# A macaron transformer block on one core: weight and bias transfers rearranged, and the order of the mixer's first jobs

## The chip, the cores and the metric

The kernel runs on one core of a Trainium2 chip. The metric is the device time of one execution in microseconds (us). Three executions of the kernel before the change took 1017.09, 1017.39 and 1017.83 us.

## What is computed

One block, for 512 tokens of width 1024, all in float32:

```python
x = x + 0.5 * swiglu(rmsnorm(x, norm_ffn1), w_gate1, w_up1, w_down1)      # d_ff = 2816
x = x + hybrid_mixer(rmsnorm(x, norm_mix), w_in, compression weights, w_out, rel_bias)
x = x + 0.5 * swiglu(rmsnorm(x, norm_ffn2), w_gate2, w_up2, w_down2)
return rmsnorm(x, norm_final)
```

The mixer projects the normalised x with `w_in` to queries, keys and values of 16 heads of width 64. Eight heads ("moba") attend over blocks; the other eight ("nsa") have three branches (compressed, selected, window), each weighted by a gate `sigmoid(h @ w)`. The compressed branch adds learned positions (`cmp_pos_k`, `cmp_pos_v`) to windows of 32 raw keys or values, and puts each window through a two-layer net (2048 to 256 with silu, 256 to 64). Every branch adds a bias that depends on the distance of the two tokens (`rel_bias`, 32 buckets).

## The kernel before

**Arithmetic.** TensorE works on float32 split into two parts: every weight and activation tile becomes a high part (`nc.scalar.activation(..., AF.Copy)` on ScalarE) and a low part (a subtraction on VectorE). A product is three matmuls (`mm3`, lines 96 to 99: high by high, high by low, low by high). In the profile these are the lines L97, L98 and L99, whatever they compute. The split of a weight tile is `halves` (L77 to L94): `whi` on ScalarE (L88), `wlo` on VectorE (L92) or, in the attention part, on GpSimd (L90).

**Order of the work.** The kernel is traced once; a scheduler with a timeline simulation sets each engine's final order and places the waits. `tc.issue_after(ins)` ties what is issued inside it behind the instruction `ins`.

**First feed-forward net** (L485 to L538). The first four of 22 blocks of 128 hidden features are computed plainly (`plain`, L254), while `sums_of_x` and `blocks_of_x` (L207 to L232) prepare sums of x for the other 18, which go in pairs by a scheme with seven products in place of eight (`pair`, L285, 14 steps to a pair). `down` (L365) adds each finished group of four blocks to x. `go` (L420) walks over the steps, and lets transfers run 12 steps ahead of the matmuls, sums 6 and splits 4. All transfers are issued by SyncE (SP in the profile). Weight chunks of 512 KB go to the buffer `raw` (`chunk`, L66, three tiles; the plain blocks' and the down projection's weights), those of 256 KB to `aw` (16 tiles; the pairs' weights). `fetch` (L60) ties each weight transfer of the nets behind the one before it, in the order of the steps:

```python
    def fetch(to, src):
        with tc.issue_after(fetched[0].ins) if fetched[0] else nullcontext():
            fetched[0] = nc.sync.dma_start(to, src)
```

**Bias tables.** `make_rows` (L466) computes the bias over the distance and writes it to DRAM (`scr_r`, `scr_c`). From there `after` (L502), called at every step, issues eight copies of 384 KB from DRAM to DRAM (`scr_t`, L518: every row 128 times, two heads to a copy) at the steps 10, 15, ... 45, and 32 small transfers of 16 KB (`cb`, L525, four at a time) at the steps 72, 80, ... 128. They wait for the rows, and are tied to nothing else. `scr_t` is read by `bias_tile` (L789) for each head of the mixer, `cb` by `cmp_pair` (L919).

**Between net and mixer.** `then` (L532) runs for each of the eight tiles of x when the last down projection is added: it adds (L483), makes the mixer's input (`gained`, L140) and squares (L154). `rms` (L165) turns the sum of squares into 1/rms: matmuls into `pr` (L171), a square root into `rc` on ScalarE (L173; one value to a token), a reciprocal on VectorE (L174), transposes into `pR` (L177), and a copy to `R` (L178; the same values along the free axis).

**The mixer's first jobs.** `stream` (L770) takes a list of jobs, each with a weight chunk and a body of matmuls, and loads two jobs ahead. `pre` (L957) is the list until attention begins: `kproj` and `vproj` (projections, 24 matmuls of 512 columns), `vn` (three chunks of a projection whose last 24 columns are the gates), `khid` and `vhid` (four chunks each of the first layer of the compression net, about 8 matmuls of 256 columns to a chunk of 512 KB), `vm` (four chunks, 24 matmuls of 512 columns each), `ksec` and `vsec` (the second layer), `proj(10)` and `proj(12)`. Behind `kproj` and `vproj`, `blocks` (L668) multiplies by R (L570), adds the positions in eight additions of 64x248, four on GpSimd and four on VectorE (L676), into a tile that it takes from `raw`, and splits the result (`ak`, L682 and L683); only then can `khid` and `vhid` begin. `vn` ends with splits scaled by `rc` (L648, L649) and with the gates, a sigmoid on ScalarE (L651); `vm` uses the same PSUM banks.

**The rest.** Attention and the output projection are interleaved by a paced loop (L1016); the second feed-forward net has the first one's form; the final norm follows.

Of the kernel before, what the change touches and what calls it, by code (L numbers as in the profile page):

```python
# [9 lines left out]
F32 = mybir.dt.float32  # L10
F32R = mybir.dt.float32r
AF = mybir.ActivationFunctionType
# [8 lines left out]
NT = S // 128  # L21
# [3 lines left out]
RVW = 384  # L25
# [4 lines left out]
def block_kernel(ctx: ExitStack, tc: tile.TileContext, A: dict, out: bass.AP):  # L30
# [26 lines left out]

    fetched = [None]

    def fetch(to, src):  # L60

        with tc.issue_after(fetched[0].ins) if fetched[0] else nullcontext():
            fetched[0] = nc.sync.dma_start(to, src)


    def chunk(shape):  # L66
        raw = wp.tile([128, 1024], F32, name="raw", tag="raw", bufs=3)
        return raw[:, :shape[0] * shape[1]].rearrange("p (a b) -> p a b", a=shape[0])

    def load(src):  # L70
# [90 lines left out]
            nc.vector.tensor_tensor(acc, acc, s, ALU.add)  # L161

    summed = [None]

    def rms(ptag):  # L165


        with tc.high_priority():
            p = pt(ptag, "pr")
            for i in range(NT):  # L170
                summed[0] = nc.tensor.matmul(p[:, i:i + 1], acc[:, i * 128:(i + 1) * 128], ones_f[:, 0:1],  # L171
                                             start=True, stop=True)
            nc.scalar.activation(rc, p[:, :NT], AF.Sqrt, bias=eps, scale=1.0 / D)  # L173
            nc.vector.reciprocal(rc, rc)  # L174
            p = pt(ptag, "pR")
            for i in range(NT):
                nc.tensor.transpose(p[:, i * 128:(i + 1) * 128], rc[:, i:i + 1].to_broadcast([128, 128]), ident)  # L177
            nc.scalar.activation(R, p, AF.Copy)  # L178


    HT = S // 2
# [1 line left out]
    class Ffn:  # L183
# [70 lines left out]
        def plain(self, f):  # L254

            got = {}

            def loads(m):
                if first_w:
                    got[m] = first_w.pop(0)  # L260
                else:
                    got[m] = chunk((8, 128))
                    fetch(got[m], self.w[m][f])

            def halves_of(m):
                got[m] = halves(got[m])

            def run(m):
                p = got["p", m] = pt(None, "pgu")
                with tc.issue_after(summed[0].ins) if (f, m) == self.behind_rms else nullcontext():  # L270
                    for k in range(NK):
                        mm3(p, got[m][k], self.xg[k], k == 0, k == NK - 1)

            def finish():
                t = [self.t("t") for _ in range(2)]
                for m in range(2):
                    nc.vector.tensor_tensor(t[m], got["p", m], R, ALU.mult)
                nc.scalar.activation(t[0], t[0], AF.Silu)
                nc.vector.tensor_tensor(t[1], t[1], t[0], ALU.mult)
                self.kept(f, t[1])  # L280

            return [[lambda m=m: loads(m), None, lambda m=m: halves_of(m), lambda m=m: run(m), finish if m else None]
                    for m in range(2)]

        def pair(self, f):  # L285
# [52 lines left out]

            def c21(m):
                if m == 0:  # L340
                    nc.scalar.activation(out[0, 1][:, :HT], bank[0, "u"], AF.Silu, scale=-1.0)
                else:
                    gate, up = out[0, 1], out[1, 1]
                    nc.vector.scalar_tensor_tensor(up[:, :HT], bank[1, "u"], -1.0, gate[:, :HT], ALU.mult, ALU.mult)
                    nc.vector.scalar_tensor_tensor(up[:, HT:], up[:, HT:], -1.0, gate[:, HT:], ALU.mult, ALU.mult)
                    self.kept(f + 1, up)
# [138 lines left out]
    with ExitStack() as ph:  # L485
# [16 lines left out]
        def after(i):  # L502
            if i == 1:
                with tc.issue_after(made[0].ins):
                    for k in range(NK):
                        squares(hp, k, "h", 16)
                rms(None)
            if i == 3:
                make_rows()
            if 3 <= i < 7:  # L510
                ffn.sums_of_x(i - 3)
            if i == 7:
                for k in range(4):
                    ffn.blocks_of_x(k)
            if 10 <= i < 50 and i % 5 == 0:
                h = slice(2 * (i // 5) - 4, 2 * (i // 5) - 2)
                row = scr_r[h]
                nc.sync.dma_start(scr_t[h].rearrange("h p w -> p h w"),  # L518
                                  bass.AP(tensor=row.tensor, offset=row.offset,
                                          ap=[[0, 128], [RVW, 2], [1, RVW]]))  # L520
            if i >= 70 and i % 8 == 0 and (i - 72) // 8 < 8:
                a = (i - 72) // 8
                row = scr_c[0:1, :]
                for j in range(NT):
                    nc.sync.dma_start(  # L525
                        cb[a * 16:(a + 1) * 16, j],
                        bass.AP(tensor=row.tensor, offset=row.offset + 31 - 8 * j - a,
                                ap=[[CMW, 16], [16 * CMW, 8], [1, 32]]))

        xg = []  # L530

        def then(d, p):  # L532
            half_added(d, p)
            xg.append(gained(d, 1))
            squares(tmp, d, "tmp", 5)
# [6 lines left out]
    with ExitStack() as ph:  # L542
# [81 lines left out]
        def token_major(key, src, width, tiles):  # L624
# [5 lines left out]
            def chunk_of(k0):  # L630
                k1 = min(k0 + per, NK)

                def body(w):
# [11 lines left out]
                    for i in range(NT):  # L645
                        pv = p[i][:, :wide].rearrange("p (h c) -> p h c", c=64)
                        hi, lo = t[i][:, :, 0], t[i][:, :, 1]
                        nc.scalar.activation(hi, pv, AF.Copy, scale=rc[:, i:i + 1])  # L648
                        nc.vector.scalar_tensor_tensor(lo, pv, rc[:, i:i + 1], f32(hi), ALU.mult, ALU.subtract)  # L649
                        if wide < width:  # L650
                            nc.scalar.activation(gates[:, i], p[i][:, wide:width], AF.Sigmoid,  # L651
                                                 scale=rc[:, i:i + 1])
                    got[key] = t
                return src[:, k0:k1], body
            return [chunk_of(k0) for k0 in range(0, NK, per)]
# [8 lines left out]
        def compress(which):  # L664
# [3 lines left out]
            def blocks(p):  # L668
# [4 lines left out]
                for g in range(2):  # L673
                    for l in range(2):
                        for e in range(2):
                            (nc.gpsimd if g == l else nc.vector).tensor_tensor(  # L676
                                xv[half(l), 8 * e:8 * e + 8, g, 0:31], tv[half(g), l:16:2, e:e + 31],
                                pos[half(g), which, 16 * e + l:16 * e + 16:2].unsqueeze(2).to_broadcast([64, 8, 31]),
                                ALU.add)
# [87 lines left out]
                    squares(tmp, d, "t", 6)  # L767
            return A["w_o"][d][:, k0:k1], body

        def stream(jobs, ahead=2):  # L770

            loaded = []
            for j in range(len(jobs) + ahead):
# [129 lines left out]
        def cmp_pair(pair):  # L903
# [38 lines left out]
            def values():  # L942
# [11 lines left out]
        vproj, vhid, vsec = compress(1)  # L954
        vn = token_major("vn", A["w_n"], 280, vn_tiles)
        vm = token_major("vm", A["w_v"], 512, vm_tiles)
        pre = [kproj, *vn, proj(10, nsa_k("ks")), *khid[:2], vm[0], *khid[2:], vproj, vm[1], ksec,  # L957
               *vhid[:2], vm[2], *vhid[2:], vm[3], vsec, proj(12, nsa_q(0))]
        fill = [proj(11, nsa_k("kw")), *[proj(12 + i, nsa_q(i)) for i in range(1, 4)]]
        for i in range(4):  # L960
            fill += [proj(2 * i, moba_t("q", i)), proj(2 * i + 1, moba_t("k", i))]
# [223 lines left out]
```

## Time and profile before

| | |
|---|---|
| median of three executions | 1017.39 us |
| the profiled execution, its own time | 1020.17 us |
| its span in the profile | 1018.4 us |
| TensorE (PE) busy | 987.1 us, 97% |
| VectorE (DVE) busy | 775.5 us, 76% |
| ScalarE (ACT) busy | 565.2 us, 56% |
| GpSimd (POOL) busy | 146.9 us, 14% |
| DMA moved | 104.53 MB, mean 103 GB/s |
| mean granted TensorE clock | 0.992 of full |

The span is the time between the first and the last instruction of the profiled execution; 1.77 us of its own time lie around it. The first net runs until about 360 us, the mixer's first jobs from 365 to about 440, attention and output projection until about 655, the second net until about 1000. An engine's idle time costs something only where the end of the kernel hangs on that engine.

### The profile page before, as it was taken

The numbers are of one execution on the slowest core, as the hardware profiler recorded it, in microseconds if no ns is written. First come the engines' busy times: TensorE is split into PE (matmuls) and PEld (weight loads), VectorE is DVE, ScalarE is ACT, GpSimd is POOL, SyncE is SP. The second block draws the span as 40 slices with busy tenths as digits, with TensorE's granted clock in tenths as the row PEclk, the third lists the DMA queues.
The fourth block names the chain that finished last, engine by engine and source line by source line (L and its number), as shares of the span: only waits on it lengthen the run. The fifth ranks groups of instructions, "written<-read, shape, count | busy, mean of one in ns | idle before, by whom it ended". The sixth has DMA issues, their size and how long they took to land.

```text
span 1018.4 us, 17022 instructions
## 1 busy us (share of the span) xinstructions
PE 987.1 (97%) x6080; PEld 873.4 (86%) x6080; DVE 775.5 (76%) x1568; ACT 565.2 (56%) x1180; POOL 146.9 (14%) x203
## 2 busy tenths in 40 slices
PE   9989999999999998999999999999999999999996
PEld 6778899999999886787878888788899999999995
DVE  6788788887677477666888978679988887776744
ACT  6453554554444256566777777656365544444435
POOL 0000000000000001126555677300000000000002
PEclk9999999999999999999999999999999999999998
DMA  6483442232411224641111322335245332441102
GB/s 222 135 283 106 144 135 91 88 105 92 124 43 42 65 58 144 189 129 53 32 32 38 95 67 79 99 111 185 99 128 157 110 99 89 125 125 42 53 11 83
DMA packets 53513, 104.53 MB, mean 103 GB/s; under 512 B 10513, under 2 KB 19170, under 8 KB 53428
## 3 DMA queue, kind: packets, MB, share of 16 engines
q1 hardware_dynamic: 53428, 103.44, 32.8%
q8 instruction: 48, 0.79, 0.3%
q14 instruction: 37, 0.30, 0.1%
HBM read 97.98 MB, written 5.30 MB: 101 GB/s over the span
## 4 chain that ended last, share of the span: by engine, by line
PE 83%; DMA 7%; DVE 5%; ACT 2%; issue 1%; SPq 1%; POOL 0%; ACTq 0%; DVEq 0%; POOLq 0%
PE pd L99 7%; PE pd L98 7%; PE pd L97 7%; PE pu L97 7%; PE pu L99 6%; PE pu L98 6%; PE pw L97 5%; PE pw L99 5%; PE pw L98 5%; PE ps_t L878 3%; PE pp L97 3%; PE pp L98 3%; PE pp L99 3%; PE pv L97 2%; PE pv L99 2%; PE pv L98 2%
## 5 line engine op out<-in xcount | busy, mean ns | idle before, releaser
L222 ACT ACTIVATE sph<-aw 128x512 fp32r<-128x512 f32 x252 | 156.2, 628 | 145.3 <-PE pu L98 61.8
L88 ACT ACTIVATE whi<-raw 128x512 fp32r<-128x512 f32 (+2 forms) x216 | 125.1, 589 | 154.6 <-PE pd L98 71.7
L223 DVE TENSOR_TENSOR spl<-aw,sph 128x512 fp32r<-128x512 f32 x252 | 170.3, 685 | 45.8 <-ACT sph L222 44.1
L98 PE MATMUL pd<-h,whi 128*128 128x512 f32 x336 | 132.6, 395 | 0.3 <-DVE h L251 0.3
L99 PE MATMUL pd<-h,wlo 128*128 128x512 f32 x336 | 131.3, 392 | 1.5 <-DVE wlo L92 1.5
L97 PE MATMUL pd<-h,whi 128*128 128x512 f32 x336 | 129.8, 394 | 3.0 <-ACT h L250 3.0
L92 DVE TENSOR_TENSOR wlo<-raw,whi 128x512 fp32r<-128x512 f32 (+1 forms) x166 | 110.3, 674 | 27.9 <-ACT whi L88 26.4
L299 DVE TENSOR_TENSOR aw<-aw 128x512 f32<-128x512 f32 x144 | 97.8, 685 | 34.7 <-DMA aw<-in_wg 16.5
L97 PE MATMUL pu<-th,sph 128*128 128x256 f32 x432 | 121.5, 281 | 1.1 <-DVE t L335 1.1
L99 PE MATMUL pu<-th,spl 128*128 128x256 f32 x432 | 121.2, 281 | 0.0
L98 PE MATMUL pu<-tl,sph 128*128 128x256 f32 x432 | 121.2, 280 | 0.0
L483 DVE SCALAR_TENSOR_TENSOR x<-pd,x 128x512 f32<-128x512 f32 x88 | 60.3, 687 | 49.1 <-PE pd L99 48.9
L97 PEld LDWEIGHTS pu<-th,sph 128*128 128x128 f32 x432 | 81.6, 189 | 2.8 <-DVE t L335 1.5
L98 PEld LDWEIGHTS pu<-tl,sph 128*128 128x128 f32 x432 | 82.0, 190 | 1.1
L97 PE MATMUL pw<-xo,sph 128*128 128x256 f32 x288 | 80.9, 282 | 1.1 <-ACT sph L222 1.1
L99 PEld LDWEIGHTS pu<-th,spl 128*128 128x128 f32 x432 | 81.2, 188 | 0.2
L98 PE MATMUL pw<-xo,sph 128*128 128x256 f32 x288 | 80.6, 281 | 0.0
L99 PE MATMUL pw<-xo,spl 128*128 128x256 f32 x288 | 79.8, 281 | 0.2 <-DVE spl L223 0.2
L99 PEld LDWEIGHTS pd<-h,wlo 128*128 128x128 f32 x336 | 63.6, 189 | 14.8 <-DVE wlo L92 1.7
L97 PEld LDWEIGHTS pd<-h,whi 128*128 128x128 f32 x336 | 62.9, 188 | 14.7 <-ACT h L250 3.4
L98 PEld LDWEIGHTS pd<-h,whi 128*128 128x128 f32 x336 | 63.9, 190 | 11.7 <-DVE h L251 1.1
L788 POOL MEMSET tb<- 128x256 f32 x16 | 4.9, 312 | 357.0 <-PE pu L99 350.7
(244 smaller groups left out, 2515.1 us busy)
## 6 DMA issues: line engine op xcount, KB each, us to landing
aw<-in_wg SPq DMA_DIRECT2D x72, 256.0 KB, 3.3
aw<-in_wu SPq DMA_DIRECT2D x72, 256.0 KB, 3.8
raw<-in_wd1a SPq DMA_DIRECT2D x20, 512.0 KB, 5.4
raw<-in_wd2a SPq DMA_DIRECT2D x20, 512.0 KB, 5.0
raw<-in_w_a SPq DMA_DIRECT2D x16, 512.0 KB, 3.6
raw<-in_w SPq DMA_DIRECT2D x8, 512.0 KB, 4.3
raw<-in_w_o SPq DMA_DIRECT2D x32, 128.0 KB, 2.2
raw<-in_wg SPq DMA_DIRECT2D x7, 512.0 KB, 3.6
```

Of the source, the lines that this page charges most:

```text
L88: nc.scalar.activation(hi, v, AF.Copy)
L92: nc.vector.tensor_tensor(lo, v, f32(hi), ALU.subtract)
L97: nc.tensor.matmul(p, w[0], v[0], start=first, stop=False, skip_group_check=again)
L98: nc.tensor.matmul(p, w[0], v[1], start=False, stop=False, skip_group_check=again)
L99: nc.tensor.matmul(p, w[1], v[0], start=False, stop=last, skip_group_check=again)
L222: nc.scalar.activation(hi, v, AF.Copy)
L223: nc.vector.tensor_tensor(lo, v, f32(hi), ALU.subtract)
L299: nc.vector.tensor_tensor(to, x, y, op)
L483: nc.vector.scalar_tensor_tensor(xs[d], p, 0.5, xs[d], ALU.mult, ALU.add)
L788: nc.gpsimd.memset(t[:, :S - 256], 0.0)
L878: nc.tensor.transpose(p[:, wide:wide + 128], lps[qi][:, j * 128:(j + 1) * 128], ident)
```

## The change

Seven edits: (1) the bias copies are tied behind the weight transfer fetched last, and the large ones are issued from step 20 to step 55 instead of 10 to 45; (2) `raw` has four tiles instead of three; (3) `stream` loads three jobs ahead instead of two; (4) a one-column square root is put behind the net's last silu, when the first tile of x is finished, so that the load of ScalarE's square-root table belongs there; (5) the gates' sigmoid is tied behind the copy of 1/rms to `R`; (6) all eight additions of the positions are on VectorE; (7) `pre` is reordered.

```diff
+    def behind_fetched():
+        return tc.issue_after(fetched[0].ins) if fetched[0] else nullcontext()
...
-        raw = wp.tile([128, 1024], F32, name="raw", tag="raw", bufs=3)
+        raw = wp.tile([128, 1024], F32, name="raw", tag="raw", bufs=4)
...
+    turned_R = [None]
...
-            nc.scalar.activation(R, p, AF.Copy)
+            turned_R[0] = nc.scalar.activation(R, p, AF.Copy)
...
-            if 10 <= i < 50 and i % 5 == 0:
-                h = slice(2 * (i // 5) - 4, 2 * (i // 5) - 2)
+            if 20 <= i < 60 and i % 5 == 0:
+                h = slice(2 * (i // 5) - 8, 2 * (i // 5) - 6)
                 row = scr_r[h]
-                nc.sync.dma_start(scr_t[h].rearrange("h p w -> p h w"),
+                with behind_fetched():
+                    nc.sync.dma_start(scr_t[h].rearrange("h p w -> p h w"),
...
+                with behind_fetched():
+                    for j in range(NT):
+                        nc.sync.dma_start(
+                            cb[a * 16:(a + 1) * 16, j],
...
         def then(d, p):
+            if d == 0:
+                with tc.issue_after(ffn.silu.ins):
+                    nc.scalar.activation(rc[:, 0:1], eps, AF.Sqrt)
...
-                            nc.scalar.activation(gates[:, i], p[i][:, wide:width], AF.Sigmoid,
-                                                 scale=rc[:, i:i + 1])
+                            with tc.issue_after(turned_R[0].ins):
+                                nc.scalar.activation(gates[:, i], p[i][:, wide:width], AF.Sigmoid,
+                                                     scale=rc[:, i:i + 1])
...
-                            (nc.gpsimd if g == l else nc.vector).tensor_tensor(
+                            nc.vector.tensor_tensor(
...
-        def stream(jobs, ahead=2):
+        def stream(jobs, ahead=3):
...
-        pre = [kproj, *vn, proj(10, nsa_k("ks")), *khid[:2], vm[0], *khid[2:], vproj, vm[1], ksec,
-               *vhid[:2], vm[2], *vhid[2:], vm[3], vsec, proj(12, nsa_q(0))]
+        pre = [kproj, *vn, proj(10, nsa_k("ks")), vm[0], *khid[:2], vm[1], *khid[2:], vproj, ksec, vm[2],
+               *vhid[:2], vm[3], *vhid[2:], vsec, proj(12, nsa_q(0))]
```

`ffn.silu` is the silu instruction traced last; the diff sets it in `plain` and in `c21`.

## Rows read from the trace of the kernel before

**Rows 1.** Waits of TensorE, 50 to 150 us: who waited for whom, total, times, longest.

```profile
PE pd L97 <- ACT h L250: 3.0, 1, 3.0
PE pd L99 <- DVE wlo L92: 1.5, 1, 1.5
PE pu L97 <- DVE t L335: 1.1, 1, 1.1
PE pw L97 <- ACT sph L222: 1.1, 1, 1.1
```

**Rows 2.** Waits of TensorE, 375 to 445 us, same columns.

```profile
PE pc L694 <- issue: 3.5, 1, 3.5
PE pc L694 <- DVE ak L683: 1.9, 1, 1.9
PE pp L97 <- ACT whi L88: 0.7, 1, 0.7
PE pc L693 <- DVE wlo L92: 0.5, 1, 0.5
```

**Rows 3.** Stretches: length, busy of PE, PEld, DVE, ACT, POOL, clock, DMA share, GB/s.

```profile
70.00:75.00 5.00, 4.88 (x14) 3.65 (x15) 5.00 (x11) 2.52 (x7) 0.00 (x0) 0.66 0.92 296
...
420.00:425.00 5.00, 5.00 (x21) 4.29 (x20) 1.86 (x3) 1.78 (x4) 0.00 (x0) 0.74 0.95 296
```

**Rows 4.** SyncE's transfer issues in order of time: start us, us, what, count.

```profile
43.25 0.66 SPq L518 DMA_DIRECT2D scr_t<-scr_r  x1
...
49.45 0.86 SPq L63 DMA_DIRECT2D raw<-in_wd1a  x1
...
58.08 0.35 SPq L63 DMA_DIRECT2D raw<-in_wd1a  x1
59.88 0.83 SPq L63 DMA_DIRECT2D aw<-in_wg  x2
```

**Rows 5.** The chain that ended last, 49 to 60 us: start us, us, what.

```profile
49.45 10.42 DMA raw<-in_wd1a
```

**Rows 6.** VectorE in order of time, start us, us; in brackets the idle time before.

```profile
68.18 0.69 DVE L299 TENSOR_TENSOR aw<-aw 128x512 f32<-128x512 f32 x1 [3.96 <-DMA aw<-in_wg]
```

**Rows 7.** The same stretch view, 150 to 350 us.

```profile
150.00:350.00 200.00, 200.00 (x1373) 185.86 (x1373) 146.24 (x256) 93.20 (x179) 0.00 (x0) 1.00 0.27 82
```

**Rows 8.** Waits of VectorE, 112 to 350 us, for transfers of the pairs' weights.

```profile
DVE aw L299 <- DMA aw<-in_wg: 5.3, 4, 3.4
```

**Rows 9.** The transfers that read the large bias table.

```profile
L789 SPq DMA_DIRECT2D tb<-scr_t x16: 326/327/537, 351.9 to 611.7; - x16
```

**Rows 10.** TensorE in order of time, from the first jobs of the mixer.

```profile
389.68 0.39 PE L99 MATMUL pp<-xo,wlo 128*128 128x512 f32 x1
393.55 0.35 PE L694 MATMUL pc<-whi,ak 128*128 128x256 f32 x1 [3.48 <-issue]
...
410.50 0.39 PE L97 MATMUL pv<-whi,xo 128*128 128x512 f32 x1
...
415.72 0.39 PE L99 MATMUL pv<-whi,xo 128*128 128x512 f32 x1
```

**Rows 11.** ScalarE in order of time, 345 to 388 us.

```profile
350.32 0.63 ACT L88 ACTIVATE whi<-raw 128x512 fp32r<-128x512 f32 x1 [2.20 <-PE pd L98]
...
381.65 1.28 ACT L173 ACT_TABLE_LOAD   x1
...
385.73 1.28 ACT L651 ACT_TABLE_LOAD   x1
...
387.36 0.60 ACT L178 ACTIVATE R<-pR 128x512 f32<-128x512 f32 x1
```

**Rows 12.** The additions of the positions: ns min/median/max, first and last start.

```profile
L676 DVE TENSOR_TENSOR raw<-t,pos x8: 555/922/1000, 388.7 to 416.5; 64x248 f32<-64x248 f32 x8
L676 POOL TENSOR_TENSOR raw<-t,pos x8: 734/938/1190, 388.8 to 415.3; 64x248 f32<-64x248 f32 x8
```

**Rows 13.** SyncE's issue of the first chunk for vm.

```profile
384.48 0.33 SPq L72 DMA_DIRECT2D raw<-in_w_v  x1
```

More of the change, by code (lines that the diff above doesn't have):

```diff
@@ L58, in block_kernel @@
     fetched = [None]
+    def behind_fetched():
+        return tc.issue_after(fetched[0].ins) if fetched[0] else nullcontext()
     def fetch(to, src):
-        with tc.issue_after(fetched[0].ins) if fetched[0] else nullcontext():
+        with behind_fetched():
             fetched[0] = nc.sync.dma_start(to, src)
     def chunk(shape):
-        raw = wp.tile([128, 1024], F32, name="raw", tag="raw", bufs=3)
+        raw = wp.tile([128, 1024], F32, name="raw", tag="raw", bufs=4)
         return raw[:, :shape[0] * shape[1]].rearrange("p (a b) -> p a b", a=shape[0])
@@ L277, in finish @@
                     nc.vector.tensor_tensor(t[m], got["p", m], R, ALU.mult)
-                nc.scalar.activation(t[0], t[0], AF.Silu)
+                self.silu = nc.scalar.activation(t[0], t[0], AF.Silu)
                 nc.vector.tensor_tensor(t[1], t[1], t[0], ALU.mult)
@@ L340, in c21 @@
                 if m == 0:
-                    nc.scalar.activation(out[0, 1][:, :HT], bank[0, "u"], AF.Silu, scale=-1.0)
+                    self.silu = nc.scalar.activation(out[0, 1][:, :HT], bank[0, "u"], AF.Silu, scale=-1.0)
                 else:
@@ L514, in after @@
                     ffn.blocks_of_x(k)
-            if 10 <= i < 50 and i % 5 == 0:
-                h = slice(2 * (i // 5) - 4, 2 * (i // 5) - 2)
+            if 20 <= i < 60 and i % 5 == 0:
+                h = slice(2 * (i // 5) - 8, 2 * (i // 5) - 6)
                 row = scr_r[h]
-                nc.sync.dma_start(scr_t[h].rearrange("h p w -> p h w"),
-                                  bass.AP(tensor=row.tensor, offset=row.offset,
-                                          ap=[[0, 128], [RVW, 2], [1, RVW]]))
+                with behind_fetched():
+                    nc.sync.dma_start(scr_t[h].rearrange("h p w -> p h w"),
+                                      bass.AP(tensor=row.tensor, offset=row.offset,
+                                              ap=[[0, 128], [RVW, 2], [1, RVW]]))
             if i >= 70 and i % 8 == 0 and (i - 72) // 8 < 8:
@@ L523, in after @@
                 row = scr_c[0:1, :]
[L524 to L528, printed above, removed]
+                with behind_fetched():
+                    for j in range(NT):
+                        nc.sync.dma_start(
+                            cb[a * 16:(a + 1) * 16, j],
+                            bass.AP(tensor=row.tensor, offset=row.offset + 31 - 8 * j - a,
+                                    ap=[[CMW, 16], [16 * CMW, 8], [1, 32]]))
         xg = []
         def then(d, p):
+            if d == 0:
+                with tc.issue_after(ffn.silu.ins):
+                    nc.scalar.activation(rc[:, 0:1], eps, AF.Sqrt)
             half_added(d, p)
```

## The prediction

> **What bounds the kernel now.** The page comes first: TensorE is busy for 987.1 of 1018.4 us and the chain that ended last is mostly matmuls, so only idle time or slow clock on TensorE can be won, some 31 us of it, and much of that lies at the two ends and in attention, which the change hardly touches. Next come TensorE's own waits, stretch by stretch. Between 50 and 150 us there are four [rows 1]: 3.0 us for the high part of a hidden tile, 1.5 us for a low part of a weight tile, and two of 1.1 us. In the mixer's first jobs there are four more [rows 2]: 3.5 us in front of khid, 1.9 us in front of vhid, and 0.7 and 0.5 us for splits of weights in between. Then the view of stretches, for the clock: between 70 and 75 us the granted clock is 0.66 of full, which is some microseconds at the lower level of 1.2 GHz after the idle time of 3.0 us; between 420 and 425 us it is 0.74, after the idle time of 1.9 us [rows 3]. Five microseconds at 0.66 lose 5 x 0.34 = 1.7 us, at 0.74 they lose 5 x 0.26 = 1.3 us. I call the places A (3.0 + 1.7 + 1.5 = 6.2 us), C (1.1 + 1.1 = 2.2), E (3.5), F (0.7 + 0.5 = 1.2) and G (1.9 + 1.3 = 3.2).
>
> **A: where it comes from.** SyncE issues the eight copies from 43.25 us on, ahead of the net's weights. The chunk for the down projection that is issued behind them at 49.45 us takes 10.42 us to land [rows 4, 5]. SyncE also stands still: the next chunk is issued at 58.08 us, and only then, at 59.88 us, the first pair's weights, because the list of fetches is in order and three raw tiles let a chunk go only when an earlier one has been split. VectorE then idles 3.96 us for these weights [rows 6], and ScalarE, held in the same way, makes the hidden tile's high part too late for TensorE.
>
> **The change, part by part.**
>
> *Copies behind the weights, and a fourth raw tile (edits 1, 2).* With four tiles each chunk goes when the one before it goes now: the last at 49.45 instead of 58.08 us, the pairs' weights about 10 us earlier, with no copy ahead of them. The wait at 68 us falls away. What is late next is VectorE: it is busy for all of 70 to 75 us [rows 3], and the low part that TensorE waits for in A's second wait stands in that backlog. So TensorE gains no more than VectorE's idle time: 3.96 us. Ends: 0 (VectorE's order becomes worse, or the clock falls at the new wait as it did at the old one) and 6.2 us (its order brings that low part forward). I take **4.0**, as VectorE's row is the nearest.
>
> *The copies in their new place.* From the first copy's issue to the landing of the chunk behind them, 16.6 us pass for 8 x 384 + 512 KB [rows 4, 5]; by size that is 1.8 us for each copy. They now stand among the pairs' weights, one about every five steps, roughly from 60 to 165 us, and the transfers queued on SyncE behind each can be late by up to 1.8 us. What waits for those is VectorE's sums (L299). From 150 to 350 us TensorE never idles [rows 7], though from 112 us on VectorE waits for these weights up to 3.4 us at a time [rows 8]: a copy there costs nothing. The copies near C, where VectorE has no such reserve, cost something: two at 0.6 us. Ends: 8 x 1.8 = 14.4 us lost, and C's 2.2 us won, should the earlier start carry that far. I take **-1.2**. The reader of the copies comes at 351.9 us [rows 9], long after. The 32 small transfers hold 16 KB each, and come four at a time at every eighth step: 0, hidden by the same reserve.
> By ring order alone, the sum would end on the other side (see the fourth case). The Trainium skill, "DMA: Bandwidth & Descriptors", section "Queues, rings and completion order", says that on each DMA engine descriptors are consumed in ring order, which speaks against putting copies between weights on one queue; the trace agrees for the chunk that took 10.42 us, and shows no case yet with single copies.
>
> *Order of the jobs (edit 7), at E.* One vm chunk moves between proj(10) and khid. It is 24 matmuls from 410.50 to 415.72 us, so 5.4 us with the last one's own 0.23 [rows 10]; the idle time is 3.5 us. The chain to khid before: R is copied at 387.36 us (0.60 long), TensorE restarts at 393.55 [rows 10, 11], 5.6 us, of which the additions take 4 x 0.94 = 3.8 us. With eight additions on VectorE (edit 6) they take 8 x 0.555 = 4.4 us at the shortest duration, and 8 x 0.92 = 7.4 at the median [rows 12]; VectorE's last addition starts at 416.5 us, over a microsecond after GpSimd's last one, so I take the shortest for that without GpSimd, 4.4: the chain is 6.2 us (at most 9.2). Edits 4 and 5 take two table loads of 1.28 us out of R's way [rows 11], so R is ready at 385.4, or at 387.96 if that fails. khid can then start at 391.6 (at worst 397.2), and TensorE is covered from 390.07 to 395.5. So edits 4 to 6 are worth nothing by themselves while vm[0] covers them; without that cover R's 2.6 us would be on the path. The table load's new place is in ScalarE's idle time, 2.20 us before 350.32 [rows 11]. The gates now come behind R, and vm needs their PSUM banks: the same ScalarE work in another order, done by 388.3 as now. vm's weights are issued at 384.48 us now [rows 13]; in the new list they are two jobs earlier and have a tile more. **+3.5**; ends 0 and 3.5.
>
> *F.* The waits are for splits of khid's weights. Loading three jobs ahead, and 5.4 us of vm matmuls in between, should remove most: **+0.8**; ends -0.5 (another job waits in its place) and 1.2.
>
> *G.* Before and after, one vm chunk stands between vproj and vhid, so the cover is the same 5.4 us. The additions start when vproj's product is scaled and take 4.4 us; now the two engines end after about 4.6 (VectorE starts late). I give 0.7 us of the 1.9, and half of the clock's 1.3: **+1.3**; ends -0.7 (VectorE's other work is put in front of the eight) and 3.2.
>
> *Sum:* 4.0 - 1.2 + 3.5 + 0.8 + 1.3 = **8.4 us**. The profiled execution took 1020.17 us (span 1018.4), so it would take 1011.8. The median of 1017.39 is 2.8 lower, so I forecast **1009.0 us** against it.
>
> **The rivals.**
> 1. *Everything goes*: A, E, F and G all vanish, clock included: 6.2 + 3.5 + 1.2 + 3.2 = 14.1, 1003.3 us. For it: none of the waits has a need of its own. Against it: VectorE's full backlog at A and the unchanged cover at G.
> 2. *Only the mixer gains*: VectorE's backlog, or one new idle time with a slow clock behind it, eats A. 3.5 + 0.8 + 1.3 = 5.6, 1011.8 us. For it: VectorE is full from 70 to 75 us. Against it: 3.96 us of its idle time go. The change not doing what it says ends here too: if the scheduler still puts copies ahead of the pairs' first weights, A stays.
> 3. *The gains cancel*: vm's first weights stay late (issued at 384.48, some microseconds to land and split), E gives 2.6 instead of 3.5, G loses 0.7, A and F give nothing and the copies cost 1.9: 1017.4 us. For it: the end values exist. Against it: four of them must come together.
> 4. *Slower, by the copies*: each of the eight holds up the weights behind it for its whole 1.8 us, and TensorE feels it. 14.4 against 4.0 + 3.5 + 0.8 + 1.3 = 9.6 is a loss of 4.8: 1022.2 us. It decides from 1.2 us of each copy on. For it: the 10.42 us. Against it: from 150 us on TensorE has no idle time beside VectorE's waits of up to 3.4 us.
>
> **How the numbers follow.** Forecast 0.50; everything 0.14; only the mixer 0.18; cancel 0.09; slower 0.09. About 0.2% (2 us) is what a measurement of this kernel can tell from no change. The first three cases are faster by more: 0.82; then 0.09 and 0.09. The range leaves out the last two, 0.18, and takes in the first rival's 1003.3 at its low end: 1002.5 to 1016 us.
>
> **What would show it.** *Edits 1, 2:* the first weights of a pair issued near 50 us, no `scr_t` copy before them, no VectorE wait of 4 us, and TensorE's wait for the hidden tile gone; a wait of some 2 us for a low part of weights may be left. *The copies:* waits of L299 for weights between 85 and 165 us grow, with none or little on TensorE. *E:* pv matmuls follow the pp matmuls directly, and TensorE has no wait of over 1 us in front of khid. *Edits 4, 5:* a table load near 350 us, none right before the square root, and R's copy ahead of the gates. *Edit 6:* eight additions near 0.55 us each. *G:* a wait of about 1.2 us is left. The prediction is wrong if TensorE has new idle time between 85 and 165 us that waits for weights, if khid still waits for the positions, or if attention, whose fill jobs now load one further ahead, gains or loses more than 2 us of idle time.

## The result, and the profile after

Four executions of the changed kernel have a median of 1009.28 us (1007.42 to 1011.25), four of the kernel before, in turn with them, 1017.61 us: the ratio is 0.9919, with a 95% interval of 0.9896 to 0.9942. The forecast of 8.4 us less compares with 8.3 measured. A later batch, four executions of the changed kernel (f1 below) and eleven of the kernel before, gave 0.990 (0.9885 to 0.9915), which is 10.3 us. That the total came so close to the forecast is partly luck: it hides errors of opposite sign, and the stages show them.

The profiled execution of after took 1011.25 us, its span is 1009.5 us (before: 1020.17 and 1018.4). The first view is again that of TensorE's waits from 50 to 150 us (who waited for whom, total us, times, longest).

```profile
PE pu L100 <- DVE t L339: 1.1, 1, 1.1
PE pd L102 <- DVE wlo L95: 0.6, 1, 0.6
PE pw L100 <- DVE x L487: 0.5, 1, 0.5
PE pd L101 <- DVE h L255: 0.3, 1, 0.3
```

The 3.0 us for the hidden tile have become 0.3, and the 1.5 us for the low part of weights 0.6 [rows 1]. The view of stretches (length, busy of PE, PEld, DVE, ACT, POOL, clock, DMA share, GB/s) shows that the clock no longer falls there; from 410 us on it does.

```profile
70.00:75.00 5.00, 3.84 (x17) 2.80 (x16) 5.00 (x10) 2.36 (x5) 0.00 (x0) 1.00 0.00 0
...
410.00:415.00 5.00, 3.57 (x21) 2.99 (x20) 4.93 (x13) 2.79 (x8) 0.00 (x0) 0.85 0.28 79
415.00:420.00 5.00, 5.00 (x23) 4.18 (x22) 2.42 (x4) 2.08 (x4) 0.00 (x0) 0.80 0.84 259
```

SyncE's issues in order of time: the pairs' weights go out from 48.87 us on instead of 59.88, and the first copy follows them [rows 4].

```profile
48.46 0.36 SPq L66 DMA_DIRECT2D raw<-in_wd1a  x1
48.87 0.90 SPq L66 DMA_DIRECT2D aw<-in_wg  x2
...
59.22 1.00 SPq L66 DMA_DIRECT2D aw<-in_wu  x2
60.57 0.66 SPq L523 DMA_DIRECT2D scr_t<-scr_r  x1
```

The mixer's first jobs: TensorE's waits from 375 to 445 us.

```profile
PE pck L101 <- DVE hl L726: 0.9, 1, 0.9
PE pck L102 <- DVE w2l L732: 0.6, 1, 0.6
PE pp L102 <- DVE wlo L95: 0.4, 1, 0.4
```

khid's wait of 3.5 us and vhid's of 1.9 us are gone [rows 2]; a new one stands in front of ksec, which now follows vproj directly. TensorE and ScalarE in order of time, the two ends of the moved cover and the steps of edits 4 and 5:

```profile
384.58 0.39 PE L102 MATMUL pp<-xo,wlo 128*128 128x512 f32 x1
384.81 0.39 PE L100 MATMUL pv<-whi,xo 128*128 128x512 f32 x1
...
390.25 0.28 PE L704 MATMUL pc<-whi,ak 128*128 128x256 f32 x1
```

```profile
343.05 1.28 ACT L541 ACT_TABLE_LOAD   x1
...
376.06 0.26 ACT L177 ACTIVATE rc<-pr,eps 128x4 f32<-128x4 f32 x1 [0.28 <-PE pr L175]
...
380.05 0.61 ACT L182 ACTIVATE R<-pR 128x512 f32<-128x512 f32 x1
380.68 1.28 ACT L661 ACT_TABLE_LOAD   x1
381.97 0.80 ACT L661 ACTIVATE gates<-pv,rc 128x24 f32<-128x24 f32 x4
```

The vm chunk fills the time from pp to khid without a gap. The square root finds its table loaded, and R comes before the gates' table load. R is ready at 380.66 us, the positions are added behind it, and khid starts at 390.25. VectorE in the same stretch shows edit 6, and what it brought:

```profile
381.72 4.33 DVE L686 TENSOR_TENSOR raw<-t,pos 64x248 f32<-64x248 f32 x8
...
387.29 0.75 DVE L693 TENSOR_TENSOR ak<-raw,ak 128x256 fp32r<-128x256 f32 x2
...
407.24 4.29 DVE L686 TENSOR_TENSOR raw<-t,pos 64x248 f32<-64x248 f32 x8
411.56 0.29 DVE L726 TENSOR_TENSOR hl<-pct,hh 128x128 fp32r<-128x128 f32 x1
411.76 0.68 DVE L95 TENSOR_TENSOR wlo<-raw,whi 128x512 fp32r<-128x512 f32 x1
412.36 0.28 DVE L732 TENSOR_TENSOR w2l<-w,w2h 128x128 fp32r<-128x128 f32 x1
```

Eight additions take 4.3 us, as predicted (4.4). The first inputs of khid (`ak`) are done at 388.04 us, 2.2 us before the cover ends at 390.25. In the second group, `hl` and `w2l`, which ksec needs, stand behind them.

**By stages.** The stages are cut at TensorE's own matmuls: the start of the first net's 51st matmul, the end of its last `pd`, the first `ps_c` (end of the first jobs), the last `ps_s` (end of the first long part of attention), the first `pgu` of the second net, the end of the last matmul. All in us, from the profiled execution of each kernel (the runs are explained below).

| kernel | to 51st matmul | net 1 | first jobs | attention | between | net 2 | end |
|---|---|---|---|---|---|---|---|
| before | 20.0 | 345.5 | 104.8 | 160.5 | 27.7 | 351.8 | 1010.3 |
| after | 20.3 | 340.1 | 98.8 | 161.5 | 26.9 | 353.7 | 1001.3 |
| after, again (f1) | 21.6 | 339.7 | 97.2 | 161.4 | 26.9 | 352.6 | 999.4 |
| e1 copies untied | 20.0 | 344.8 | 98.8 | 161.1 | 26.2 | 354.4 | 1005.3 |
| e2 three raw tiles | 20.6 | 342.0 | 99.0 | 160.9 | 26.4 | 352.0 | 1000.8 |
| e3 old job list | 19.4 | 339.2 | 102.6 | 160.8 | 26.9 | 352.4 | 1001.3 |
| e4 kw job ahead | 19.9 | 341.0 | 103.3 | 165.1 | 27.2 | 353.0 | 1009.5 |
| e5 held tile | 19.0 | 339.5 | 98.8 | 161.7 | 26.9 | 352.7 | 998.7 |
| e6 no edits 4, 5 | 21.4 | 341.5 | 98.6 | 160.8 | 26.9 | 351.3 | 1000.4 |
| e7 positions on both | 19.5 | 339.3 | 96.8 | 161.2 | 27.6 | 353.1 | 997.5 |
| e8 ksec later | 22.2 | 340.1 | 96.9 | 161.8 | 26.2 | 354.2 | 1001.4 |
| f2 copies doubled | 19.7 | 342.1 | 97.3 | 160.9 | 26.9 | 351.7 | 998.5 |
| f3 = e7 + e5 | 21.9 | 339.3 | 96.8 | 161.3 | 27.3 | 353.0 | 999.5 |
| f4 = e7 + e8 + e5 | 20.6 | 340.4 | 97.3 | 161.3 | 27.7 | 353.7 | 1001.0 |

Two things scatter from execution to execution, whatever the edit. The 51st matmul starts between 19.0 and 22.2 us. And a wait of TensorE is followed by a spell at the lower clock in one profile and not in another: stretches of 1 us show 0.50 for some 3.4 us, which loses about 1.7 us. The wait at 411 us is followed by one in after, e1 and e5, not in f1, with the same waits. So a stage is compared with its spells counted: first jobs take 97.2 us in f1 and 97.1 in after (98.8 - 1.7); before, 103.1 (104.8 - 1.7). Net 1 holds a spell in before, in e6, and in e1 one of twice the length; attention one in f1, e3, e5 and e8; "between" one in before, e2, e7 and f4.

### The profile page after: what moved, and what is told of

Its sections match the earlier page's. It is cut to its first block, busy times and chain, and to the rows that moved or that the text cites. A ratio compares the mean times of both kernels' runs of the same rounds, so it can differ in the third digit from the quotient of the medians.

```text
span 1009.5 us, 17013 instructions
## 1 busy us (share of the span) xinstructions
PE 983.8 (97%) x6080; PEld 871.0 (86%) x6080; DVE 776.9 (77%) x1578; ACT 564.9 (56%) x1181; POOL 137.3 (14%) x193
## 4 chain that ended last, share of the span: by engine, by line
PE 82%; DVE 11%; DMA 3%; issue 2%; ACT 1%; POOL 0%; SPq 0%; DVEq 0%; ACTq 0%; POOLq 0%
PE pd L102 6%; PE pd L100 6%; PE pd L101 6%; PE pu L100 6%; PE pu L102 5%; PE pu L101 5%; PE pw L100 4%; PE pw L101 4%; PE pw L102 4%; PE pp L102 3%; PE pgu L100 3%; PE pp L100 3%; PE pp L101 3%; PE pgu L101 3%; PE pv L100 3%; PE pgu L102 3%
## 5 line engine op out<-in xcount | busy, mean ns | idle before, releaser
L303 DVE TENSOR_TENSOR aw<-aw 128x512 f32<-128x512 f32 x144 | 97.6, 683 | 31.7 <-DMA aw<-in_wg 13.6
L100 PEld LDWEIGHTS pw<-xo,sph 128*128 128x128 f32 x288 | 54.1, 188 | 2.6 <-ACT sph L226 1.6
```

Of the source, the lines that this page charges most:

```text
L100: nc.tensor.matmul(p, w[0], v[0], start=first, stop=False, skip_group_check=again)
L303: nc.vector.tensor_tensor(to, x, y, op)
```

## The experiments

Each is one edit of the changed kernel. Runs e1 to e4 share one chip and the kernel before on it (median 1018.34 us), e5 to e8 another (1018.31), f1 to f4 a third batch (1019.13).

**e1: copies untied, in their old place, four raw tiles** (the 32 small transfers untied in the same way).

```diff
-            if 20 <= i < 60 and i % 5 == 0:
+            if 10 <= i < 50 and i % 5 == 0:
...
-                with behind_fetched():
...
```

> The changed kernel (1009.3 us), with the bias copies as before: from step 10, tied to nothing; the fourth raw tile stays. Theory 'tile': place A was won by the fourth tile, since the pairs' weights are issued at 48.9 instead of 59.9 us and have time to land even behind the copies: 1009 to 1011 us, VectorE's wait for them under 1.5 us. Theory 'copies': A was won because no 3.1 MB of copies stand ahead of the weights: 1013 to 1015 us, with a wait of VectorE of 3 us or more for the first pair's weights and an idle time of 2 us or more on TensorE near 67 us.

Measured: 1015.19 us, ratio 0.9962 (0.9946 to 0.9979). The longest of TensorE's waits from 50 to 150 us, and the stretches behind it:

```profile
PE pd L101 <- DVE h L255: 5.3, 1, 5.3
```

```profile
70.00:75.00 5.00, 0.93 (x2) 0.83 (x3) 5.00 (x11) 0.52 (x2) 0.00 (x0) 0.81 0.21 35
75.00:80.00 5.00, 5.00 (x14) 3.95 (x13) 5.00 (x10) 3.12 (x6) 0.00 (x0) 0.51 0.23 35
```

The fourth tile alone brings 0.7 us of net 1 (344.8 for 345.5). The pairs' weights go out at 50.49 us, 9 us earlier than before, but right behind the copies, and TensorE waits longer than it did. The tie is worth 4.7 us of net 1 (344.8 to 340.1). So theory 'copies' holds for the total and for TensorE, but not in the way that it gave: VectorE never waits 3 us at a time. Its three waits in front of TensorE's are 0.30, 0.66 and 1.78 us, 2.7 in all. VectorE in order of time:

```profile
69.64 0.69 DVE L303 TENSOR_TENSOR aw<-aw 128x512 f32<-128x512 f32 x1 [1.78 <-DMA cb<-scr_c]
...
70.92 2.49 DVE L227 TENSOR_TENSOR spl<-aw,sph 128x512 fp32r<-128x512 f32 x4
73.33 0.68 DVE L255 TENSOR_TENSOR h<-t,h 128x512 fp32r<-128x512 f32 x1
```

The same rows in after:

```profile
67.96 0.67 DVE L255 TENSOR_TENSOR h<-t,h 128x512 fp32r<-128x512 f32 x1
...
69.23 2.48 DVE L227 TENSOR_TENSOR spl<-aw,sph 128x512 fp32r<-128x512 f32 x4
```

In e1 the scheduler put four splits of the pairs' weights (`spl`), 2.4 us, in front of `h`, on which TensorE waits; in after, and before, they stand behind it. By these rows about half of the 5.3 us is late transfers and half VectorE's order. The profile puts the longest wait for a transfer down to a small one (`cb`); e1 unties these too, so it does not tell the large copies from the small.

**e2: three raw tiles, copies tied.**

```diff
-        raw = wp.tile([128, 1024], F32, name="raw", tag="raw", bufs=4)
+        raw = wp.tile([128, 1024], F32, name="raw", tag="raw", bufs=3)
```

> The changed kernel with three raw tiles instead of four. Theory 'copies': A stays won, since the pairs' weights, though issued near 58 us, land in 3 to 4 us with nothing ahead of them; the end of the first net is within 1.5 us of the changed kernel's. Theory 'tile': A comes back, 3 us or more at the end of the first net. Both: the mixer's first jobs lose 1 to 2 us to weights that come later. Theory 'tile costs in the second net' (2.0 us are lost there in the changed kernel): those 2 us come back, since this kernel's order there is that of before. Sum: 1007 to 1011 us for 'copies', 1011 to 1015 for 'tile'.

Measured: 1011.03 us, ratio 0.9934 (0.9913 to 0.9954). The longest of TensorE's waits, 50 to 150 us, and VectorE in order of time:

```profile
PE pd L101 <- DVE h L255: 2.8, 1, 2.8
```

```profile
68.40 2.49 DVE L227 TENSOR_TENSOR spl<-aw,sph 128x512 fp32r<-128x512 f32 x4
70.81 0.68 DVE L255 TENSOR_TENSOR h<-t,h 128x512 fp32r<-128x512 f32 x1
```

A wait of 2.8 us for the hidden tile is back, but not for want of weights: the pairs' weights go out at 52.65 us, and VectorE is busy for all of 58 to 80 us. Again the four splits stand in front of `h`. Net 1 takes 342.0 us: of the gain of 5.4 us, the tie without the tile gives 3.5, the tile behind it 1.9, which is over the 1.5 of 'copies' and under the 3 of 'tile'. These shares belong to the kernels as scheduled: neither e1 nor e2 keeps VectorE's order. The first jobs take 99.0 us without a spell, 1.8 more than f1, as was expected of three tiles. Net 2 takes 352.0 us, as before.

**e3: the old job list.**

```diff
-        pre = [..., vm[0], *khid[:2], vm[1], *khid[2:], vproj, ksec, vm[2], ...
+        pre = [..., *khid[:2], vm[0], *khid[2:], vproj, vm[1], ksec, *vhid[:2], vm[2], ...
```

> The changed kernel with the old list of jobs (khid directly behind proj(10), vm[1] ahead of ksec). If vm[0] covers the chain to khid: that idle time is back, though shorter than the 3.5 us of before, since R is copied about 2.5 us earlier: 2 to 3 us; 1011.5 to 1013.5 us in all. Rival, that the early R alone is enough: no idle time of over 1 us in front of khid, 1008 to 1010.5 us.

Measured: 1011.34 us, ratio 0.9939 (0.9924 to 0.9954). TensorE's waits, 375 to 430 us, and TensorE in order of time:

```profile
PE pv L100 <- ACT whi L91: 2.0, 1, 2.0
PE pc L704 <- DVE ak L693: 1.9, 1, 1.9
```

```profile
382.82 0.39 PE L102 MATMUL pp<-xo,wlo 128*128 128x512 f32 x1
385.16 1.96 PE L100 MATMUL pv<-whi,xo 128*128 128x512 f32 x4 [1.96 <-ACT whi L91]
386.91 0.42 PE L704 MATMUL pc<-whi,ak 128*128 128x256 f32 x1
```

The first jobs take 102.6 us with a spell behind each wait, 3.4 us in all, so 99.2 without spells, against 97.1 to 97.2. The new list is worth about 2 us of waiting, and up to 5.4 with the spells. The wait of 2.0 us does not stand in front of khid (`pc`): the scheduler put four matmuls of a vm chunk (`pv`) ahead of khid, and they wait for the split of their weights. khid itself starts 3.7 us after the last `pp` has ended, where it was 3.5 before. So the early R did not shorten the time until khid can start, and the rival falls.

**e4: the projection for kw, from the jobs that fill attention, placed ahead of ksec as cover.**

```diff
+               proj(11, nsa_k("kw")), ksec, vm[2],
...
-        fill = [proj(11, nsa_k("kw")), *[proj(12 + i, nsa_q(i)) for i in range(1, 4)]]
+        fill = [proj(12 + i, nsa_q(i)) for i in range(1, 4)]
```

> The changed kernel with the job proj(11) moved from attention's filling jobs up between vproj and ksec: 24 more matmuls (5.4 us) of cover where the changed kernel idles 1.4 us and then runs at the lower clock (1.7 us lost). Theory 'cover': both go and nothing else changes: 1005.5 to 1007 us. Rival 'moved': the filling job is missing in attention, where TensorE then idles as much more: 1008 to 1010.5 us, with the first jobs free of waits of over 0.5 us in either case.

Measured: 1020.39 us, ratio 1.0023 (1.0011 to 1.0035): slower than the kernel before by 0.2%, and outside both expectations. The wait in front of ksec did not go; ScalarE came late instead (it had idled 4.67 us for the transfer of ksec's weights), and waits of TensorE appeared inside attention, of which one line each:

```profile
PE pck L100 <- ACT w2h L731: 2.5, 1, 2.5
...
PE ps_s L864 <- DVE m L870: 2.0, 8, 0.5
```

In after these waits for `m` are six, of 1.1 us together. Attention became 3.6 us longer (165.1 for 161.5), although a job of 5.4 us had been taken out of it; the first jobs, which took that job in, grew by 4.5. A filling job in attention is not spare work to be moved at will.

**e5: four tiles, one of them held by GpSimd through the second net.**

```diff
+        held = wp.tile([128, 1024], F32, name="held", tag="raw", bufs=4)
+        nc.gpsimd.memset(held[:, 0:1], 0.0)
         ffn.lay(A["wd2a"])
         ffn.go(after)
+        nc.gpsimd.tensor_copy(held[:, 1:2], held[:, 0:1])
```

> The changed kernel, but one of the four raw tiles is held by a dummy through the second net, so that the net has three, with the instruction order of the changed kernel unaltered on TensorE, VectorE and ScalarE. The changed kernel loses 2.0 us between the second net's first matmul and its end, the kernel with three raw tiles 0.3 us. Theory 'transfers' (weights that come earlier land in each other's way, or their splits come in front of urgent ones): the loss goes to 0.5 us or less, 1007 to 1008.5 us in all on the first chip, a ratio near 0.990. Rival 'order' (the scheduler's order for four tiles is the worse one, whatever the transfers do): the loss stays at 1.5 us or more, ratio 0.992 or higher.

Measured: 1008.43 us, ratio 0.9907 (0.9894 to 0.9920). Net 2 takes 352.7 us, inside the scatter of the kernels with four free tiles (351.3 to 354.4). The pairs' weights still go out at 684.20 us (after: 685.89, e2: 692.83), so holding the tile did not bring the old order back, and the run does not decide what the second net lost.

**e6: without edits 4 and 5.**

```diff
-            if d == 0:
-                with tc.issue_after(ffn.silu.ins):
-                    nc.scalar.activation(rc[:, 0:1], eps, AF.Sqrt)
...
-                            with tc.issue_after(turned_R[0].ins):
```

> The changed kernel without the early square root and without the tie of the gates behind R. As the prediction has it, vm[0] covers the chain to khid: R comes about 3 us later, khid's inputs near 390.5 instead of 387.7 us on the changed kernel's clock, against a cover that ends at 390.2: no wait or one of up to 1 us, ratio to the changed kernel 1.000 to 1.001. Rival 'the early R carries E': a wait of 2 us or more in front of khid, 2 us or more slower.

Measured: 1010.60 us, ratio 0.9924 (0.9909 to 0.9939). One wait comes to those of after:

```profile
PE pc L699 <- DVE wlo L95: 1.1, 1, 1.1
```

The first jobs take 98.6 us without a spell, 1.4 more than f1. The rival falls: no wait of 2 us stands in front of khid. The two edits are worth 1 us or so, mostly hidden by vm[0]; the ratios do not separate it from nothing.

**e7: the positions on both engines, as before the change.**

```diff
-                            nc.vector.tensor_tensor(
+                            (nc.gpsimd if g == l else nc.vector).tensor_tensor(
```

> The changed kernel with the positions on GpSimd and VectorE again. Eight additions on VectorE took 4.3 us in both places; the two engines side by side took 3.3 us on VectorE and 3.8 on GpSimd. Theory 'neutral': each addition goes back to about 0.9 us, the end of the eight comes 0.3 to 0.6 us earlier, the rest is hidden: within 1 us of the changed kernel. Rival 'VectorE freed was the gain': over 1 us slower.

Measured: 1007.93 us, ratio 0.9901 (0.9887 to 0.9914), the lowest time of the study. The additions (ns min/median/max, first and last start), here and in after, in that order:

```profile
L686 DVE TENSOR_TENSOR raw<-t,pos x8: 575/978/1015, 380.1 to 408.5; 64x248 f32<-64x248 f32 x8
L686 POOL TENSOR_TENSOR raw<-t,pos x8: 854/971/1123, 380.2 to 408.1; 64x248 f32<-64x248 f32 x8
```

```profile
L686 DVE TENSOR_TENSOR raw<-t,pos x16: 559/572/590, 381.7 to 411.0; 64x248 f32<-64x248 f32 x16
```

From the first start to the last end on both engines, a group here takes 3.9 us at 380 and 4.3 at 405, where VectorE starts half a microsecond behind GpSimd; eight on VectorE alone take 4.3 in both places. So edit 6 makes each addition faster and the first group 0.4 us longer. The wait for `hl` falls from 0.9 to 0.4 us. The Trainium skill, "GPSIMD Engine Reference", section "8. Key points", says that GpSimd shares its SBUF interfaces with VectorE and contends with VectorE instructions that have two SBUF inputs; these additions have two, and the trace agrees: 0.572 us alone, 0.978 beside GpSimd.

**e8: ksec one job later, behind vm[2].**

```diff
-        pre = [..., vproj, ksec, vm[2], ...
+        pre = [..., vproj, vm[2], ksec, ...
```

> The changed kernel with ksec behind vm[2] instead of in front of it, so that TensorE does not stand in the chain of ksec at 411 us (0.9 and 0.6 us, with 1.7 us at the lower clock behind). If the wait is ksec's own: it goes, with the clock's loss, 2 to 3 us faster than the changed kernel. Rival: vhid's inputs (the positions of vproj) are ready at 412.6 us in any case, 1.7 us after the cover ends, so the wait only changes its name: within 1 us of the changed kernel.

Measured: 1009.40 us, ratio 0.9917 (0.9903 to 0.9931). The rival holds: the wait got another name, that of before:

```profile
PE pc L704 <- DVE ak L693: 1.9, 1, 1.9
```

Either ksec or vhid stands too close behind vproj; one vm chunk covers one of them.

**f1: the changed kernel again, as the control.**

> The changed kernel once more, unaltered, as the control of this batch. Its median should fall within 1.5 us of 1009.3. Theory 'clock': the spread of its executions (1007.4 to 1011.3) comes from spells at the lower clock behind short idle times of TensorE, 1.8 us each, that come in one execution and not in the next; then the profile has the same waits as the first one (1.1 us in front of pu near 98 us, 1.5 us in front of the split products of hl and w2l near 411 us), but not necessarily a clock of 0.5 behind the latter. Rival 'transfers': the spread comes from weights that land late in net 1; then the waits themselves change by a microsecond or more.

Measured: 1008.85 us (1008.56 to 1009.36), ratio 0.990 (0.9885 to 0.9915). The waits are those of the first profile but for 1.4 us in front of `pu`, and the clock stays up behind the one at 411 us:

```profile
410.00:415.00 5.00, 3.56 (x23) 2.82 (x22) 4.94 (x13) 2.37 (x8) 0.00 (x0) 1.00 0.14 24
415.00:420.00 5.00, 5.00 (x28) 4.27 (x27) 3.59 (x7) 2.85 (x5) 0.00 (x0) 1.00 0.82 289
```

Theory 'clock' holds for that place, the only stage in which the two profiles of this one kernel differ by more than 1.5 us; the start and net 2 differ by 1.3 and 1.1 us, which 'clock' does not explain.

**f2: each copy issued twice.**

```diff
+    scr_t2 = dp.tile([16, 128, RVW], F32, name="scr_t2")
...
                 with behind_fetched():
-                    nc.sync.dma_start(scr_t[h].rearrange("h p w -> p h w"),
+                    for to in scr_t, scr_t2:
+                        nc.sync.dma_start(to[h].rearrange("h p w -> p h w"),
...
```

> Each of the eight tied copies is issued twice, the second into a scratch tensor of the same size that nobody reads: eight more transfers of 384 KB among the weights of net 1. Theory 'hidden': the copies cost nothing where they are now, because VectorE's and the raw tiles' reserve takes them up; then net 1 ends within 1 us of where it ends in the changed kernel, the total is within 1.5 us of the control, and VectorE's waits for weights between 85 and 165 us grow by some microseconds. Rival 'priced' (the prediction's term): two of the copies cost 0.6 us each; then the doubled ones cost 1 to 3 us more, as new idle time of TensorE between 85 and 165 us. Rival 'ring': each further copy costs up to 1.8 us; then the total is 8 to 14 us above the control.

Measured: 1010.53 us, ratio 0.9918 (0.9901 to 0.9935), 1.7 above the control, though the two intervals overlap. TensorE's waits, 50 to 170 us:

```profile
PE pu L100 <- DVE t L339: 2.7, 1, 2.7
PE pv L102 <- DVE spl L227: 1.1, 1, 1.1
PE pu L100 <- DVE t L348: 0.7, 1, 0.7
```

Net 1 takes 342.1 us, 2.0 to 2.4 more than in the two profiles of after. By these profiles eight more copies cost 0.25 to 0.3 us each: 'priced' holds, 'hidden' falls by its 1 us in net 1, and 'ring' with its 8 to 14 us is excluded. VectorE's longest wait for `in_wg` from 85 to 165 us grows from 1.9 to 4.0 us; it is handed on at `t`, the place C of the prediction.

**f3: e7 and e5 together.**

> The changed kernel with the additions of positions on GpSimd and VectorE again (as before the change) and with one of the four raw tiles held by GpSimd through the second net. Theory 'additions': eight additions on VectorE delay the splits of ksec's operands; with both engines the wait in front of ksec is 1.0 us instead of 1.5, and the spell of slow clock behind it comes seldom; the gain is 0.5 to 2 us in the first jobs, as in the run with both engines alone. Theory 'tile': holding a raw tile gives back up to 0.5 us of the second net. Together 1006.5 to 1008.5 us, 1 to 2.5 below the control. Rival 'neutral': both were within the spread of the executions; then the median is within 0.7 us of the control.

Measured: 1009.37 us (1008.16 to 1009.72), ratio 0.9901 (0.9887 to 0.9915); 0.5 above the control. Rival 'neutral' holds: e7's low time does not stand out (its ratio, 0.9901, is that of f1); its profile has no spell in the first jobs and a short start. Without spells its first jobs are 0.4 us shorter (96.8 for 97.2).

**f4: e7, e8 and e5 together.**

> As the run before it, and ksec stands one job later, behind the third chunk of vm, as the cover for the splits of its operands. Theory 'additions': with ksec late the wait passes to vhid, which needs the additions; with both engines they end about 0.6 us earlier than on VectorE alone, so that of the 1.9 us in front of vhid some 1 us is left, and the total is within 1 us of the run before it. Rival 'order': the cover removes the wait altogether, and the kernel gains another 1 to 1.5 us.

Measured: 1010.25 us, ratio 0.9919 (0.9902 to 0.9937), 1.4 above the control. The wait in front of vhid is 1.5 us:

```profile
PE pc L704 <- DVE ak L693: 1.5, 1, 1.5
```

The cover does not remove it, so 'order' falls; 'additions' expected 1 us left, and a total within 1 us of f3 (it is 0.9 above). No version tried is shown to beat the changed kernel.

## Why the prediction was right, and where it was not

The total was right, 8.4 against 8.3 us (10.3 in the later batch), partly by luck. By stages the prediction gave +2.8 in net 1 (4.0 - 1.2), +5.6 in the first jobs and nothing elsewhere. The profiles of after and f1 show +5.4 and +5.8, +6.0 and +7.6, and elsewhere -2.1 and -0.9 (without the first 50 matmuls): net 1 gained twice what was forecast, and later stages gave some of it back. E, F and G as measured below add up to 4.7 and 6.4 of the first jobs' 6.0 and 7.6 us; the rest is not accounted for. The mechanisms of E and F were right, that of A in part.

- **A, mis-sized: 4.0.** From 60 to 90 us TensorE was idle for 4.5 us and lost 1.7 us to the clock before; after, it is idle for 1.5 us. (Idle is a stretch's length less PE's busy time, the clock's loss its length times what the clock lacks of 1.) That is 4.7 us. The step that failed is "TensorE gains no more than VectorE's idle time": that bounds the work moved, not the clock that came with the wait. My price for a spell, 1.7 and 1.3 us from stretches of 5 us, was right to low: the second stretch had cut the spell's beginning off. The reason given for SyncE's standstill is also incomplete. Before, it issued six of the small transfers between the two chunks of [rows 4]:

```profile
50.35 6.91 SPq L525 DMA_DIRECT2D cb<-scr_c  x6
```

The profile shows SyncE waiting 4.6 us there for the large copies. With three tiles and the tie (e2) the pairs' weights go out at 52.65 us, so most of the 11 us by which they go out earlier in after does not need the fourth tile. And e1 and e2 show a term that the text left out: in which order the scheduler puts VectorE's work.
- **The copies, mis-sized: -1.2.** At C, from 90 to 110 us, idle time went from 2.3 to 1.1 us (f1: 1.5). So the place gained about 1 us where 1.2 were to be lost; f2's price of 0.25 to 0.3 us per copy says that the copies still take something there (inferred: their own price was measured with eight more, not with none). The fourth case held that each copy delays what stands behind it by 1.8 us, 14.4 for eight; in f2 the eight further ones add 3.7 us to VectorE's waits for `in_wg` from 85 to 165 us (7.4 for 3.7) and 2.0 to 2.4 to TensorE. Ring order on each DMA engine is stated by the Trainium skill in "DMA: Bandwidth & Descriptors", section "Queues, rings and completion order". For eight copies in a row the trace agrees with it: a transfer of the pairs' weights behind them takes up to 9.1 us to land in e1, up to 7.2 in after.
- **E, right.** The vm chunk covers the way from R to khid without a gap; e3 confirms that the order is needed, for there khid again starts 3.7 us behind `pp`. The chain was mis-sized: from R's end (380.66) to khid's first inputs (388.04) it takes at least 7.4 us, not 6.2, since two other instructions of VectorE come between the additions and `ak`; the cover had room for it. "Edits 4 to 6 are worth nothing by themselves" holds only with that cover, as was written, and even then e6 finds 1.1 us of new waiting.
- **F, right in size.** Both waits are gone, and 0.4 us stands at 425 us in front of another job, as the term's lower end allowed for.
- **G, wrong in mechanism: 1.3.** vhid's wait is gone, not shortened. In its stead ksec waits 0.9 + 0.6 us, and a spell may follow (after) or not (f1): so the place wins 0.4 (3.6 to 3.2 us, spells counted) or 2.1 us; that 1.3 lies between is luck. The failed step is "before and after, one vm chunk stands between vproj and vhid": true, but ksec, which used to follow that chunk, now comes ahead of it, and `hl` and `w2l` stand in VectorE's queue behind the 4.3 us of additions. The text asked what is put in front of the additions, not what is queued behind them.
- **What was missing: the second net.** `raw` serves it too. Its pairs' weights go out at 685.89 us instead of 701.15, VectorE does sums (L303) earlier, and `h` (L255), on which `pd` waits, comes behind them. In after, of TensorE's waits from 640 to 1000 us:

```profile
PE pd L101 <- DVE h L255: 1.1, 1, 1.1
```

This line stands in every profile with four tiles; with three, the wait is 0.3 us (before) or not there (e2). The stage itself takes 352.9 us in the mean of nine profiles with four free tiles (351.3 to 354.4), 351.8 and 352.0 with three. So about 1 us seems to be lost, less than the stage's scatter of 3 us; that the order of VectorE's instructions does it is read from the trace and was not undone by a run. Why the stage scatters stays open.
- **Attention** gained nothing from loading three jobs ahead: 1.0 us more from the first `ps_c` to the last `ps_s`, 0.8 less behind it, where the kernel before has a spell that after has not.

The rivals: 'only the mixer gains' is refuted by net 1's 5.4 us and the new 70 to 75 us stretch, 'the copies' by f2, 'everything goes' by the waits left at A (0.6 us) and in front of ksec, 'the gains cancel' by the total.

## What to carry to other kernels

Here transfers that nobody needs soon cost most where the queue issued several of them in a row ahead of weights; singly among weights that are loaded ahead, eight further ones cost TensorE 0.25 to 0.3 us each, about a sixth of the 1.8 us that one takes in a row (an estimate from [rows 4, 5]). Add to the price of an idle time of TensorE a possible spell at the lower clock, and see it as a chance, from more than one profile. Where a buffer is added or a job moved, list every stage that uses the buffer and every instruction queued behind the moved work on each engine: both surprises of this case stood in such a list. And where a scheduler sets the order, an edit taken back moves other instructions too: compare the order on each engine before a wait is put down to that edit (e1, e2, e3).

## What the runs showed of the hardware

- The same waits of TensorE (0.9 and 0.6 us at 411 us) were followed by 3.4 us at the lower level of 1.2 GHz in three profiles of kernels with this stretch unaltered (after, e1, e5) and by none in f1, e6 and f2, nor in e2 (1.0 and 0.6 us). Nor was the longer wait of 2.5 us in e4, or that of 1.9 us in e8, while those of 1.9 us in before and e3 were. Two executions of one kernel can differ by about 1.7 us at such a place.
- ScalarE's table load takes 1.28 us, and the instruction behind it starts at once (380.68 + 1.28 = 381.96; the gates start at 381.97). The Trainium skill, "ScalarE: Activation LUTs", section "What ACT_TABLE_LOAD costs", adds about 1.38 us of drain; no such time shows on either side of the load here (R ends at 380.66).
- An addition of 64x248 elements with two SBUF inputs takes VectorE 0.572 us alone and 0.978 beside GpSimd's, which takes 0.971: sharing eight of them between the two engines saves 0.4 us of 4.3 where both start together, and nothing where VectorE starts half a microsecond late.
